# Streaming encoder step: squares of x summed on TensorE in four groups, roots broadcast without diagonal tiles, first weight block in product order

## The chip, the cores and the metric

The kernel runs on one core of a Trainium2 chip. The metric is the device time of one execution in microseconds (us); smaller is better. TensorE is called PE in the rows, VectorE DVE, ScalarE ACT, GpSimd POOL, and SP is the queue from which all of this kernel's transfers are issued. PEld is TensorE's loading of weights, which runs beside its matmuls.

## The reference, cut to what matters

One layer of a hybrid encoder is applied to 512 prompt tokens and 64 sample tokens, all in fp32. The change lies at its very beginning:

```python
mod = jax.nn.silu(c) @ w_ada + b_ada
shift, scale, gate = jnp.split(mod, 3, axis=-1)
h = rmsnorm(x, norm_g) * (1.0 + scale[:, None]) + shift[:, None]
proj = h @ w_in
```

`rmsnorm` divides each token by the root of the mean of its 2048 squares and multiplies by a weight. Attention, a state-space branch, a pooling branch and an output projection follow; the change does not touch them.

## The kernel before, in words

Tokens lie along the free dimension (columns 0 to 511 prompt, 512 to 575 sample: NP = 512, NT = 576), and the 2048 features in 16 blocks of 128 partitions. x arrives transposed, as eight transfers of two blocks each, into four tiles `xc` (line 92).

**The statistics** (lines 349 to 376). The 16 blocks are squared, 15 on ScalarE and the last on VectorE, and VectorE adds them into two tiles `acc`, one for the even and one for the odd blocks. Then ten matmuls (line 373) multiply five stretches of 128 tokens of both `acc` tiles with a column of ones, so that `pss` holds the sum of squares of 128 tokens per column, with the token on the partition. `rms_inv` (line 100) makes the inverse roots `r` of it: one root on ScalarE, the rest small steps on VectorE. Ahead of these matmuls twelve others (`warm`, line 368) multiply a piece of x with the identity; nothing reads their result.

**The broadcast** (lines 387 to 399). A root per partition is needed as a row on every partition. VectorE scales the identity by each column of `r` (tiles `dg`, line 391), five matmuls of ones with `dg` (lines 393 and 395) put the rows into the PSUM tile `rb`, and ScalarE copies them to `rstdx`.

**Modulation** (`ada_mm`, `ada_sel`, `modulate`). For each block b, `ada_mm(b, half)` multiplies SiLU(c) with a half of the block's 1 MB + 1 MB of `w_ada` columns, 16 matmuls in all, into `pa`. `ada_sel(b)` copies `pa` to `S` on ScalarE, transposes it with two matmuls, and reduces it on VectorE to `m4`: shift and scale of prompt and sample. `modulate(b)` forms h from x, `rstdx` and `m4`, splits it into a rounded part `hh` (ScalarE) and a remainder `hl` (VectorE), and keeps the 64 sample columns as `hs`. `split_w(b)` does the same to 768 columns of `w_in`, giving `w1h` and `w1l`.

**The first projection** (`first_tiles`, line 429). For each block, six tiles of output (fA to fD) take three products each, `w1h*hh`, `w1l*hh` and `w1h*hl`, one tile after the other, and four matmuls for the sample tokens go into `fS`. The loop of line 447 interleaves this with the next block: `fS` of block b, `ada_mm(b+1)`, the first tile, `ada_sel(b+1)`, `modulate(b+1)`, the other five tiles. `load_ada` issues the transfers two blocks ahead, in the order of the blocks.

From line 320 to the end of this stage the order on PE, DVE, ACT and SP is the order in which the code is written (`manual_schedule`). What stands in an engine's queue behind a waiting instruction waits too. The rest of the kernel comes out in the same order on every engine with the change and without it.

Of the kernel before, what the change touches and what calls it, by code (L numbers as in the profile page):

```python
# [9 lines left out]
F32 = mybir.dt.float32  # L10
F32R = mybir.dt.float32r
I32 = mybir.dt.int32
AF = mybir.ActivationFunctionType
ALU = mybir.AluOpType
# [3 lines left out]
NP = 512  # L18
NS = 64
NT = NP + NS  # L20
# [17 lines left out]
HELD = 3  # L38
LASTORD = (4, 0, 1, 2, 3)
LASTENG = ("PE", "DVE", "Activation")  # L40
WARM = 12
WLANE = 0
W1POS = 2
SPLIT0 = 1
ORDERED = ("PE", "SP", "DVE", "Activation")
# [3 lines left out]
def kernel(ctx, tc, xp, xs, xT, cT, wada_ss, wada_g, bsh, bsc, bgate, ng, wf1, wrest,  # L49
# [4 lines left out]
    V, A, G, PE, SY = nc.vector, nc.scalar, nc.gpsimd, nc.tensor, nc.sync  # L54
# [3 lines left out]
    wp = ctx.enter_context(tc.tile_pool(name="wp", bufs=3))  # L58
# [4 lines left out]
    def mul(o, a, b):  # L63
        V.tensor_tensor(o, a, b, op=ALU.mult)  # L64

    def add(o, a, b):
        V.tensor_tensor(o, a, b, op=ALU.add)  # L67

    def sub(o, a, b):
        V.tensor_tensor(o, a, b, op=ALU.subtract)  # L70

    def ts(o, a, s1_, s2_, op0, op1):
        V.tensor_scalar(o, a, s1_, s2_, op0=op0, op1=op1)
# [5 lines left out]
    ident = const.tile([128, 128], F32, name="ident")  # L79
# [3 lines left out]
    ones = onesr.bitcast(F32)  # L83
    scT = const.tile([128, KT, 2], F32, name="scT")
# [1 line left out]
    SY.dma_start(cTt, cT)  # L86
    A.activation(scT, cTt, AF.Silu)
    pre = const.tile([128, 1], F32, name="pre")
    A.activation(pre, ones[:, 0:1], AF.Sqrt)
    xc = [ck(f"xc{c}") for c in range(4)]  # L90
    for n in range(8):
        SY.dma_start(xc[n // 2][:, 2 * (n % 2):2 * (n % 2) + 2], xT[n])
# [25 lines left out]
    pp = psctx.enter_context(tc.tile_pool(name="pp", bufs=2, space=PSUM))  # L118
    pm = psctx.enter_context(tc.tile_pool(name="pm", bufs=4, space=PSUM))

    def mtile(name, shape=(128, 512)):
        return pm.tile(list(shape), F32, tag="m", name=name)
# [39 lines left out]
    hh, hl = [], []  # L162
# [161 lines left out]
    def ada_mm(b, half):  # L324
        if half == 0:
            pas[b] = mtile("pa")
        pa = pas[b]
        for k in range(8 * half, 8 * half + 8):
            g = k % 4
            PE.matmul(pa[32 * g:32 * g + 32, 0:256], sc[:, k], adat[b, k // 8][:, k % 8], start=(k < 4),  # L330
                      stop=(k >= KT - 4))

    def ada_sel(b):
        pa = pas.pop(b)
        S = s1.tile([128, 256], F32, tag="S", name="S", bufs=1)
        A.copy(S, pa[:, 0:256])
        for z in range(2):
            PE.transpose(pa[:, 256 + 128 * z:384 + 128 * z], S[:, 128 * z:128 * z + 128], ident)
        m4 = s1.tile([128, 4], F32, tag="m4", name="m4", bufs=4)
        V.tensor_reduce(out=m4.rearrange("p (z t) -> p z t", z=2), op=ALU.add, axis=mybir.AxisListType.X,  # L340
                        in_=pa[:, 256:512].rearrange("p (z g t) -> p z t g", z=2, g=4)[:, :, 0:2])
        V.tensor_scalar(m4[:, 0:2], m4[:, 0:2], prm[:, 0, b:b + 1], None, op0=ALU.add)
        ts(m4[:, 2:4], m4[:, 2:4], prm[:, 1, b:b + 1], prm[:, 2, b:b + 1], ALU.add, ALU.mult)
        m4s[b] = m4
# [1 line left out]
    for b in range(PRE):  # L346
        load_ada(b)

    acc = [wp.tile([128, NT], F32, tag="wh", name="acc") for _ in range(2)]
    for n in range(16):  # L350
        xv = xc[n // 4][:, n % 4]
        if n < 2:
            A.activation(acc[n], xv, AF.Square)
        else:
            sq = wp.tile([128, NT], F32, tag=("wl", "wr")[n % 2], name="sq")
            if n == 15 and 1:
                mul(sq, xv, xv)
            else:
                A.activation(sq, xv, AF.Square)
            if n < 16:  # L360
                add(acc[n % 2], acc[n % 2], sq)
            else:
                acc.append(sq)
    V.tensor_scalar(prm[:, 1], prm[:, 1], 1.0, None, op0=ALU.add)

    warm = pp.tile([128, 2, 512], F32, tag="pj", name="warm")
    for n in range(WARM):
        PE.matmul(warm[:, 0, 0:128], ident, xc[3][:, WLANE, 0:128], start=True, stop=True)
    pss = mtile("pss", (128, 8))
    for t in range(5):  # L370
        t0 = 128 * t if t < 4 else NT - 128
        for n, a in enumerate(acc):
            PE.matmul(pss[:, t:t + 1], a[:, t0:t0 + 128], ones[:, 0:1], start=n == 0, stop=n == len(acc) - 1)
    ada_mm(0, 0)
    ada_mm(0, 1)
    r = rms_inv(s1, pss[:, 0:5], D, None, -0.5 * EPS, [128, 5], "n")
    wsp = {}

# [5 lines left out]
        sub(wl, w, wh.bitcast(F32))  # L384
        wsp[b] = w, wh, wl

    dg = wp.tile([128, 5, 128], F32, tag="wh", name="dg")
    rb = pp.tile([128, 2, 512], F32, tag="pj", name="rb")
    rstdx = s1.tile([128, NT], F32, tag="rstdx", name="rstdx", bufs=1)
    for t in range(5):  # L390
        V.tensor_scalar(dg[:, t], ident, r[:, t:t + 1], None, op0=ALU.mult)
        if t < 4:
            PE.matmul(rb[:, 0, 128 * t:128 * t + 128], ones, dg[:, t], start=True, stop=True)
        else:
            PE.matmul(rb[:, 1, 0:64], ones, dg[:, t, 64:128], start=True, stop=True)
    split_w(0)
    ada_sel(0)
    A.copy(rstdx[:, NP:NT], rb[:, 1, 0:64])
    A.copy(rstdx[:, 0:NP], rb[:, 0])

    fA = pp.tile([128, 2, 512], F32, tag="pj", name="fA")
    fB = pp.tile([128, 2, 512], F32, tag="pj", name="fB")
# [3 lines left out]
    f1p = [fA[:, 0], fA[:, 1], fB[:, 0], fB[:, 1], fC, fD]  # L406
    blk = {}

    def modulate(b):
        m4 = m4s.pop(b)  # L410
        c, i = divmod(b, 4)
        if i == 0:
            hh.append(ck(f"hh{c}", F32R))
            hl.append(ck(f"hl{c}", F32R))
        xv = xc[c][:, i]
        hs = s1.tile([128, 64], F32, tag="hs", name="hs", bufs=3)
        parts = [(0, slice(0, NP)), (1, slice(NP, NT))]
        for t, tk in parts[::-1] if b == 0 else parts:
            stt(xv[:, tk], xv[:, tk], m4[:, 2 + t:3 + t], rstdx[:, tk], ALU.mult, ALU.mult)
            if t:  # L420
                V.tensor_scalar(hs, xv[:, NP:NT], m4[:, 1:2], None, op0=ALU.add)
        for t, tk in parts:
            A.activation(hh[c][:, i, tk], xv[:, tk], AF.Identity, bias=m4[:, t:t + 1])  # L423
        for t, tk in ((0, slice(0, NP)), (1, slice(NP, NT))):
            stt(hl[c][:, i, tk], xv[:, tk], m4[:, t:t + 1], hh[c][:, i, tk].bitcast(F32), ALU.add, ALU.subtract)
        w, wh, wl = wsp.pop(b)
        blk[b] = w, wh, wl, hs

    def first_tiles(b, fs):
        w, wh, wl, hs = blk[b]  # L430
        c, i = divmod(b, 4)
        f0, l0 = b == 0, b == KT - 1
        for f in fs:
            if f < 6:
                wsl = slice(128 * f, 128 * f + 128)
                PE.matmul(f1p[f], wh[:, wsl], hh[c][:, i, 0:NP], start=f0, stop=False)
                PE.matmul(f1p[f], wl[:, wsl], hh[c][:, i, 0:NP], start=False, stop=False)
                PE.matmul(f1p[f], wh[:, wsl], hl[c][:, i, 0:NP], start=False, stop=l0)
            else:

                for g in range(4):
                    PE.matmul(fS[32 * g:32 * g + 32], hs[:, 32 * (g // 2):32 * (g // 2) + 32],
                              w[:, 384 * (g % 2):384 * (g % 2) + 384], start=f0, stop=l0, skip_group_check=True)

    modulate(0)
    dg_ = disc()
    for b in range(KT):
        if b + PRE < KT:
            load_ada(b + PRE)
        if b + 1 < KT:  # L450
            split_w(b + 1)
        if b == KT - 2:
            for n in range(3):
                w_load()
        first_tiles(b, F1CUT[0])
        if b + 1 < KT:
            ada_mm(b + 1, 0)
            ada_mm(b + 1, 1)
        first_tiles(b, F1CUT[1])
        if b + 1 < KT:  # L460
            ada_sel(b + 1)
            modulate(b + 1)
        if b == KT - 2:
            for n in range(1):
                w_split()
        first_tiles(b, F1CUT[2])
        if b == 0:
            ssm_load()
        for _ in range(DISCN if b >= 2 else 0):
            next(dg_, None)  # L470
    for n in range(0):
# [8 lines left out]
    for f in range(6):  # L480
        PE.matmul(fT[:, 64 * f:64 * f + 64], SS[:, 128 * (f % 3):128 * (f % 3) + 128], i2[:, f // 3], start=True,
                  stop=True)
# [512 lines left out]
    for f in range(4):  # L995
        wh, wl = w_next(4)
# [19 lines left out]
        else:  # L1016
            sq = s5.tile([128, NT], F32, tag="tB", name="sq2")
# [42 lines left out]
    for t in range(5):  # L1060
        n = 128 if t < 4 else 64
# [139 lines left out]
    ws = [w_next(2) for _ in range(HELD)]  # L1201
# [3 lines left out]
    with tc.manual_schedule(engines={getattr(mybir.EngineType, e) for e in LASTENG}):  # L1205
        r = {}
# [155 lines left out]
```

## Time and profile before

| what | value |
|---|---|
| median of 3 runs | 1035.28 us (1035.24 to 1037.51) |
| the profiled execution, its own time | 1035.37 us |
| its span in the profile | 1033.1 us |
| TensorE busy | 97% of the span |
| VectorE busy | 69% |
| ScalarE busy | 45% |
| DMA busy, first tenth of the span | over 90% |

The span runs from the first to the last instruction; the execution's own time is 2.3 us longer, which lies outside it. Times in rows count from the start of the span. A row of the timeline has the start, the time that it covers, engine, line, operation, output and inputs, shapes, the number of instructions merged into it (xN), and in brackets how long its engine had been idle before and what released it. An fp32 matmul is recorded as two instructions. In a table by stretches, PEclk is the clock that TensorE was granted, as a share of 2.4 GHz.

### The profile page before, as it was taken

Reading aid. Unit: us, or ns where it says so; the run is one execution under the profiler, and the core shown is the slowest. Engines: PE = TensorE matmul, PEld = TensorE weight load, DVE = VectorE, ACT = ScalarE, POOL = GpSimd, SP = SyncE. Lnnn points to the kernel's source line nnn. Section 1 sums busy time; section 2 is a strip of 40 time slices with the busy share of each in tenths; the row PEclk is TensorE's granted clock in tenths of the full one; section 3 lists DMA queues with packets and bytes.
Section 4 is the critical chain, followed back from the end, with each engine's and each line's share of the span. In section 5 each row is a group of like instructions: output and inputs, shape, how many; then the busy total and the mean of one; then the engine's idle time right before and its main releaser. Section 6 shows DMA issues by size and latency. Waiting matters only on the chain. (4 is left out here: it accounts for less than half of the span.)

```text
span 1033.1 us, 17910 instructions
## 1 busy us (share of the span) xinstructions
PE 1003.0 (97%) x7048; PEld 905.1 (88%) x7048; DVE 710.7 (69%) x1678; ACT 460.3 (45%) x913; POOL 4.2 (0%) x36
## 2 busy tenths in 40 slices
PE   4999999999999999999999999999999999999996
PEld 3666689999999999999989999999999888888885
DVE  5677785745555564644599798886354679988776
ACT  5332365635454544543744454557452514232325
POOL 0000000000000000000000000000000000000000
PEclk9999999999999999999999999999999999999999
DMA  9999552232233333222223222221322585746425
GB/s 366 413 416 369 232 172 86 88 103 87 85 99 94 99 97 95 74 74 75 72 62 91 84 62 86 77 65 51 112 72 87 191 295 195 236 151 197 149 92 194
DMA packets 51571, 148.44 MB, mean 144 GB/s; under 512 B 9312, under 2 KB 18528, under 8 KB 46816
## 3 DMA queue, kind: packets, MB, share of 16 engines
q1 hardware_dynamic: 51488, 147.31, 42.5%
q8 instruction: 55, 0.90, 0.3%
q14 instruction: 28, 0.23, 0.1%
HBM read 137.75 MB, written 9.53 MB: 143 GB/s over the span
## 5 line engine op out<-in xcount | busy, mean ns | idle before, releaser
L500 PE MATMUL pj<-hh,wh 128*128 128x288 f32 x1344 | 299.0, 304 | 0.0
L500 PE MATMUL pj<-hh,wl 128*128 128x288 f32 x1344 | 287.8, 296 | 0.0
L500 PE MATMUL pj<-hl,wh 128*128 128x288 f32 x1344 | 287.4, 295 | 0.0
L500 PEld LDWEIGHTS pj<-hh,wh 128*128 128x128 f32 x1344 | 214.5, 189 | 4.9 <-issue 0.8
L500 PEld LDWEIGHTS pj<-hh,wl 128*128 128x128 f32 x1344 | 216.0, 188 | 0.1
L500 PEld LDWEIGHTS pj<-hl,wh 128*128 128x128 f32 x1344 | 215.6, 188 | 0.1
L146 ACT CAST wh<-w 128x1024 fp32r<-128x1024 f32 x120 | 125.8, 1049 | 198.0 <-PE po L1122 89.4
L70 DVE TENSOR_TENSOR wl<-w,wh 128x1024 fp32r<-128x1024 f32 x120 | 146.7, 1223 | 93.9 <-ACT wh L146 92.9
L1119 PE MATMUL po<-wl,yh 128*128 128x512 f32 (+1 forms) x256 | 99.1, 387 | 0.0
L1120 PE MATMUL po<-wh,yl 128*128 128x512 f32 (+1 forms) x256 | 99.0, 387 | 0.0
L1118 PE MATMUL po<-wh,yh 128*128 128x512 f32 (+1 forms) x256 | 98.7, 387 | 0.0
L76 DVE SCALAR_TENSOR_TENSOR acc<-ada,scT,acc 128x512 f32<-128x512 f32 x120 | 82.9, 744 | 0.5
L621 ACT ACTIVATE P<-P,s 128x128 f32<-128x128 f32 (+4 forms) x80 | 43.3, 541 | 77.2 <-DVE s L620 76.9
L618 DVE CUSTOM_DVE_ANT_0 P<-sps,Tb 128x128 f32<-128x128 f32 (+4 forms) x80 | 36.6, 458 | 36.5 <-PE sps L614 22.4
L1119 PEld LDWEIGHTS po<-wl,yh 128*128 128x128 f32 x256 | 48.1, 188 | 9.9
L1118 PEld LDWEIGHTS po<-wh,yh 128*128 128x128 f32 x256 | 48.1, 188 | 9.9
L1120 PEld LDWEIGHTS po<-wh,yl 128*128 128x128 f32 x256 | 48.1, 188 | 9.8
L622 DVE RECIPROCAL s<-s 128x1 f32<-128x1 f32 (+1 forms) x80 | 12.8, 161 | 43.1 <-ACT P L621 42.4
L623 DVE TENSOR_SCALAR P<-P,s 128x128 f32<-128x128 f32 (+4 forms) x80 | 29.5, 370 | 2.3
L423 ACT ACTIVATE hh<-xc,m 128x512 fp32r<-128x512 f32 (+1 forms) x32 | 15.4, 529 | 34.4 <-DVE xc L76 34.4
L67 DVE TENSOR_TENSOR ssqa<-ssqa,sq 128x576 f32<-128x576 f32 x7 | 5.3, 757 | 35.7 <-ACT sq L666 35.7
L70 DVE TENSOR_TENSOR K<-kv,K 64x704 fp32r<-64x704 f32 x32 | 28.3, 883 | 0.6
(338 smaller groups left out, 1423.6 us busy)
## 6 DMA issues: line engine op xcount, KB each, us to landing
w<-in_wrest_dram SPq DMA_DIRECT2D x84, 512.0 KB, 3.7
ada<-in_wada_ss_dram SPq DMA_DIRECT2D x22, 1024.0 KB, 8.6
w<-in_wout_dram SPq DMA_DIRECT2D x32, 512.0 KB, 3.7
ada<-in_wada_g_dram SPq DMA_DIRECT2D x32, 512.0 KB, 4.3
adac<-in_wada_ss_dram SPq DMA_DIRECT2D x10, 1024.0 KB, 13.8
w<-in_wf_dram SPq DMA_DIRECT2D x16, 384.0 KB, 11.0
xc<-in_xT_dram SPq DMA_DIRECT2D x8, 576.0 KB, 7.3
Tb<-in_ext_dram SPq DMA_DIRECT2D x8, 512.0 KB, 3.6
```

What stands on the lines that cost most here:

```text
L70: V.tensor_tensor(o, a, b, op=ALU.subtract)
L76: V.scalar_tensor_tensor(o, in0=a, scalar=s, in1=b, op0=op0, op1=op1)
L146: A.copy(wh, t)
L423: A.activation(hh[c][:, i, tk], xv[:, tk], AF.Identity, bias=m4[:, t:t + 1])
L500: PE.matmul(ps[:, ch, 0:HC], ws[:, k % 8], hs[c][:, i, HC * ch:HC * ch + HC], start=(k == 0 and first), stop=(k == KT - 1 and last))
L618: V.tensor_tensor_reduce(out=p[0:n, 0:nk], in0=ps[0:n], in1=Tb[0:n, h, ::-1][:, b0:b0 + nk], scale=1.0, scalar=-3.0e38, op0=ALU.add, op1=A ...
L621: A.activation(p[0:n, 0:nk], p[0:n, 0:nk], AF.Exp, bias=s4[0:n, 1:2], accum_out=s4[0:n, 2:3])
L622: V.reciprocal(s4[0:n, 3:4], s4[0:n, 2:3])
L623: V.tensor_scalar(p[0:n, 0:nk], p[0:n, 0:nk], s4[0:n, 3:4], None, op0=ALU.mult)
L1118: PE.matmul(po[t], yh[c][:, ci, s_], wh[:, i], start=f0, stop=False)
L1119: PE.matmul(po[t], yh[c][:, ci, s_], wl[:, i], start=False, stop=False)
L1120: PE.matmul(po[t], yl[c][:, ci, s_], wh[:, i], start=False, stop=l0)
```

## The change

- `acc` is made four times, once for each `xc` tile: the first block of a group is squared into it, the three others are added. After each group five matmuls add its sums into `pss`, which stays open over the four groups.
- The twelve `warm` matmuls of 128 columns go. In their place stand seven of 512 columns that multiply the identity with ones (`FILL`, `WARM`): five ahead of the first group's matmuls, one ahead of the second's, one ahead of the third's.
- The early root that brings in ScalarE's table (`pre`) reads `scT` in place of `ones`.
- `dg` goes. The matmuls to `rb` take a column of `r`, repeated 128 times, as weights and the identity as the moving side.
- The second half of block 0's `ada_mm` moves behind these matmuls. VectorE multiplies block 0 of x by `rb` straight from PSUM; ScalarE's copies to `rstdx` follow, then `ada_sel(0)`, then `split_w(0)`.
- Block 0 has its own `modulate`, in which ScalarE applies scale and shift in one step from the product, and its own `first_block`: all six `w1h*hh`, then `fS` and `ada_mm(1)`, then all six `w1l*hh`, then `ada_sel(1)` and `modulate(1)`, then all six `w1h*hl`.

```diff
-WARM = 12
-WLANE = 0
+FILL = 4
+WARM = (5, 1, 1, 0)
...
-    A.activation(pre, ones[:, 0:1], AF.Sqrt)
+    A.activation(pre, scT[:, 0, 0:1], AF.Sqrt, scale=0.0)
...
-    acc = [wp.tile([128, NT], F32, tag="wh", name="acc") for _ in range(2)]
-    for n in range(16):
...
+    pss = mtile("pss", (128, 8))
+    warm = pp.tile([128, 2, 512], F32, tag="pj", name="warm")
+    for n in range(0, 16, 4):
+
+        for w in range(WARM[n // 4]):
+            PE.matmul(warm[:, 0, 0:128 * FILL], ident, ones.unsqueeze(1).to_broadcast([128, FILL, 128]), start=True,
+                      stop=True)
+        acc = wp.tile([128, NT], F32, tag="wh", name="acc")
+        for m in range(n, n + 4):
+            xv = xc[m // 4][:, m % 4]
+            if m == n:
+                A.activation(acc, xv, AF.Square)
+                continue
+            sq = wp.tile([128, NT], F32, tag=("wl", "wr")[m % 2], name="sq")
+            if m == 15:
+                mul(sq, xv, xv)
+            else:
+                A.activation(sq, xv, AF.Square)
+            add(acc, acc, sq)
+        for t in range(5):
+            t0 = 128 * t if t < 4 else NT - 128
+            PE.matmul(pss[:, t:t + 1], acc[:, t0:t0 + 128], ones[:, 0:1], start=n + t == 0, stop=n == 12,
+                      skip_group_check=True)
...
     ada_mm(0, 0)
-    ada_mm(0, 1)
     r = rms_inv(s1, pss[:, 0:5], D, None, -0.5 * EPS, [128, 5], "n")
...
-        V.tensor_scalar(dg[:, t], ident, r[:, t:t + 1], None, op0=ALU.mult)
+        rt = r[:, t:t + 1].to_broadcast([128, 128])
         if t < 4:
-            PE.matmul(rb[:, 0, 128 * t:128 * t + 128], ones, dg[:, t], start=True, stop=True)
+            PE.matmul(rb[:, 0, 128 * t:128 * t + 128], rt, ident, start=True, stop=True)
...
+    ada_mm(0, 1)
+    mul(xc[0][:, 0, 0:NP], xc[0][:, 0, 0:NP], rb[:, 0])
+    mul(xc[0][:, 0, NP:NT], xc[0][:, 0, NP:NT], rb[:, 1, 0:64])
+    A.copy(rstdx[:, 0:NP], rb[:, 0])
+    A.copy(rstdx[:, NP:NT], rb[:, 1, 0:64])
+    ada_sel(0)
     split_w(0)
-    ada_sel(0)
-    A.copy(rstdx[:, NP:NT], rb[:, 1, 0:64])
-    A.copy(rstdx[:, 0:NP], rb[:, 0])
...
+        if b == 0:
+
+            for t, tk in parts:
+                A.activation(hh[c][:, i, tk], xv[:, tk], AF.Identity, scale=m4[:, 2 + t:3 + t], bias=m4[:, t:t + 1])
+            ts(hs, xv[:, NP:NT], m4[:, 3:4], m4[:, 1:2], ALU.mult, ALU.add)
+            ts(xv[:, 0:NP], xv[:, 0:NP], m4[:, 2:3], m4[:, 0:1], ALU.mult, ALU.add)
+            sub(hl[c][:, i, 0:NP], xv[:, 0:NP], hh[c][:, i, 0:NP].bitcast(F32))
+            sub(hl[c][:, i, NP:NT], hs, hh[c][:, i, NP:NT].bitcast(F32))
+            blk[b] = *wsp.pop(b), hs
+            return
...
+    def first_block():
+
+        w, wh, wl, hs = blk[0]
+        for n, (ws, xs_) in enumerate(((wh, hh), (wl, hh), (wh, hl))):
+            for f in range(6):
+                PE.matmul(f1p[f], ws[:, 128 * f:128 * f + 128], xs_[0][:, 0, 0:NP], start=n == 0, stop=False)
+            if n == 0:
+                first_tiles(0, (6,))
+                ada_mm(1, 0)
+                ada_mm(1, 1)
+            if n == 1:
+                ada_sel(1)
+                modulate(1)
```

TensorE's order from the start to the first matmuls of block 0, before (`pss` are the sums of squares, `pa` the modulation, `fS` the sample tokens):

```order
L368 MATMUL warm<-xc_80,ident 128x128 x12
L373 MATMUL pss<-onesr,acc 128x1 x10
L330 MATMUL pa<-ada,sc 32x256 x16
L393 MATMUL rb<-dg,onesr 128x128 x4
L395 MATMUL rb<-dg,onesr 128x64
L338 MATMUL pa<-ident,S 128x128 x2
L442 MATMUL fS<-w_129,hs 32x384 x4
L330 MATMUL pa<-ada,sc 32x256 x16
L436 MATMUL fA<-hh_265,w1h 128x512
```

The same place with the change:

```order
L354 MATMUL warm<-onesr,ident 128x512 x5
L370 MATMUL pss<-onesr,acc 128x1 x5
L354 MATMUL warm<-onesr,ident 128x512
L370 MATMUL pss<-onesr,acc 128x1 x5
L354 MATMUL warm<-onesr,ident 128x512
L370 MATMUL pss<-onesr,acc 128x1 x10
L330 MATMUL pa<-ada,sc 32x256 x8
L391 MATMUL rb<-ident,r 128x128 x4
L393 MATMUL rb<-ident,r 128x64
L330 MATMUL pa<-ada,sc 32x256 x8
L338 MATMUL pa<-ident,S 128x128 x2
L461 MATMUL fA<-hh_264,w1h 128x512 x2
```

The unread matmuls now stand ahead of three of the four groups, half of the modulation behind the broadcast, and block 0 begins with its products in place of `fS`.

The rest of block 0 on TensorE with the change, up to block 1's first rows (the last two; `fS` there reads `hs` of block 1):

```order
L453 MATMUL fS<-w_129,hs 32x384 x4
L330 MATMUL pa<-ada,sc 32x256 x16
L461 MATMUL fA<-hh_264,w1l 128x512 x2
L461 MATMUL fB<-hh_264,w1l 128x512 x2
L461 MATMUL fC<-hh_264,w1l 128x512
L461 MATMUL fD<-hh_264,w1l 128x512
L338 MATMUL pa<-ident,S 128x128 x2
L461 MATMUL fA<-hl_265,w1h 128x512 x2
L461 MATMUL fB<-hl_265,w1h 128x512 x2
L461 MATMUL fC<-hl_265,w1h 128x512
L461 MATMUL fD<-hl_265,w1h 128x512
L453 MATMUL fS<-w_129,hs 32x384 x4
```

Between the transposes of block 1 (L338) and block 1's `fS` six matmuls are left, where before there were fifteen (five tiles with three products each).

ScalarE's order from the root to block 0's `hh`, before:

```order
L106 ACTIVATE s<-v 128x5
L382 CAST w1h<-w_129 128x768
L336 COPY S<-pa 128x256
L398 COPY rstdx<-rb 128x64
L399 COPY rstdx<-rb 128x512
L423 ACTIVATE hh_265<-xc_77,m_254 128x512
```

And with the change:

```order
L106 ACTIVATE s<-v 128x5
L397 COPY rstdx<-rb 128x512
L398 COPY rstdx<-rb 128x64
L336 COPY S<-pa 128x256
L380 CAST w1h<-w_129 128x768
L422 ACTIVATE hh_264<-xc_77,m_251 128x512
```

The copy of `S`, from which the modulation of block 0 is read, now stands behind both copies of the roots, and as built these wait until VectorE has read the same PSUM tile. Two more waits belong to the new code: the fourth group's `acc` takes the buffer of the first, so its first square waits for the first group's `pss` matmuls; and the first unread matmul waits for `ones`, which VectorE writes behind its second addition, as before.

## Rows read from the trace of the kernel before

**Rows 1.** The page: span, and busy time of TensorE.
```profile
span 1033.1 us, 17910 instructions
...
PE 1003.0 (97%) x7048; PEld 905.1 (88%) x7048; DVE 710.7 (69%) x1678; ACT 460.3 (45%) x913; POOL 4.2 (0%) x36
```
**Rows 2.** Busy time by stretch: length, engines, PEclk, DMA share, GB/s.
```profile
18.50:21.30 2.80, 2.54 (x27) 2.44 (x28) 0.69 (x2) 0.00 (x0) 0.00 (x0) 1.00 1.01 413
21.30:24.70 3.40, 3.40 (x34) 1.45 (x33) 2.79 (x11) 0.93 (x2) 0.00 (x0) 0.52 1.02 424
...
34.86:41.92 7.06, 7.06 (x61) 4.67 (x60) 3.80 (x10) 2.74 (x5) 0.00 (x0) 1.00 1.02 419
```
**Rows 3.** Timeline of the front: squares, additions, ones, and the last transfers of x.
```profile
7.11 1.43 DVE L67 TENSOR_TENSOR acc<-acc,sq 128x576 f32<-128x576 f32 x2 [4.15 <-ACT sq L359]
8.46 0.22 DVE L82 TENSOR_SCALAR onesr<-ident 128x128 fp32r<-128x128 f32 x1
8.76 1.28 ACT L89 ACT_TABLE_LOAD   x1
10.16 6.02 ACT L359 ACTIVATE sq<-xc 128x576 f32<-128x576 f32 x10
10.86 6.78 DVE L67 TENSOR_TENSOR acc<-acc,sq 128x576 f32<-128x576 f32 x10 [1.24 <-ACT sq L359]
15.44 0.81 SPq L189 DMA_DIRECT2D ada<-in_wada_ss_dram  x2
18.34 0.76 DVE L67 TENSOR_TENSOR acc<-acc,sq 128x576 f32<-128x576 f32 x1
```
**Rows 4.** The unread matmuls: durations in ns (min/median/max), first and last start.
```profile
L368 PEld LDWEIGHTS warm<-xc,ident x24: 192/333/333, 13.8 to 18.4; 128*128 128x128 f32 x24
```
**Rows 5.** Timeline, TensorE from the sums to block 0.
```profile
19.16 2.17 PE L373 MATMUL pss<-onesr,acc 128*128 128x1 f32 x18 [0.27 <-DVE acc L67]
21.25 3.49 PE L330 MATMUL pa<-ada,sc 128*32 128x256 f32 x32
24.67 1.25 PE L393 MATMUL rb<-dg,onesr 128*128 128x128 f32 x8
27.80 0.85 PE L442 MATMUL fS<-w,hs 128*32 128x384 f32 x8 [1.49 <-DVE hs L421]
28.47 1.91 PE L330 MATMUL pa<-ada,sc 128*32 128x256 f32 x32
34.86 0.85 PE L442 MATMUL fS<-w,hs 128*32 128x384 f32 x8
```
**Rows 6.** Timeline, the steps from sums to modulation, and in block 0 and 1.
```profile
21.36 0.17 DVE L73 TENSOR_SCALAR v<-pss 128x5 f32<-128x5 f32 x1 [2.18 <-PE pss L373]
22.43 0.17 DVE L76 SCALAR_TENSOR_TENSOR r<-s,r 128x5 f32<-128x5 f32 x1
22.63 1.07 DVE L391 TENSOR_SCALAR dg<-ident,r 128x128 f32<-128x128 f32 x5
26.23 0.59 ACT L399 COPY rstdx<-rb 128x512 f32<-128x512 f32 x1
31.12 0.38 PE L338 MATMUL pa<-ident,S 128*128 128x128 f32 x2
31.95 0.28 DVE L73 TENSOR_SCALAR m<-m,prm 128x2 f32<-128x2 f32 x1
33.26 0.25 DVE L421 TENSOR_SCALAR hs<-xc,m 128x64 f32<-128x64 f32 x1
```
**Rows 7.** Groups by form: a product out of PSUM on VectorE, and `hh`.
```profile
L64 DVE TENSOR_TENSOR tm<-po,gt 128x512 f32<-128x512 f32 x16 | 10.6, 688 | 0.4 <-PE po L1120 0.3
L423 ACT ACTIVATE hh<-xc,m 128x512 fp32r<-128x512 f32 x16 | 11.6, 724 | 34.4 <-DVE xc L76 34.4
```
**Rows 8.** Timeline, ScalarE: block 2's weights and `S`.
```profile
34.71 0.83 ACT L382 CAST w1h<-w 128x768 fp32r<-128x768 f32 x1 [0.69 <-DMA w<-in_wf_dram]
37.56 0.37 ACT L336 COPY S<-pa 128x256 f32<-128x256 f32 x1 [2.02 <-PE pa L330]
```

More of the change, by code (lines that the diff above doesn't have):

```diff
@@ L347 @@
         load_ada(b)
-    acc = [wp.tile([128, NT], F32, tag="wh", name="acc") for _ in range(2)]
-    for n in range(16):
[L351 to L356, printed above, removed]
+    pss = mtile("pss", (128, 8))
[12 more added lines that the diff above has]
+            if m == 15:
                 mul(sq, xv, xv)
@@ L359 @@
                 A.activation(sq, xv, AF.Square)
[L360 to L363, printed above, removed]
-    V.tensor_scalar(prm[:, 1], prm[:, 1], 1.0, None, op0=ALU.add)
[L366 to L373, printed above, removed]
+            add(acc, acc, sq)
[3 more added lines that the diff above has]
+                      skip_group_check=True)
+    V.tensor_scalar(prm[:, 1], prm[:, 1], 1.0, None, op0=ALU.add)
     ada_mm(0, 0)
-    ada_mm(0, 1)
     r = rms_inv(s1, pss[:, 0:5], D, None, -0.5 * EPS, [128, 5], "n")
@@ L385, in split_w @@
         wsp[b] = w, wh, wl
-    dg = wp.tile([128, 5, 128], F32, tag="wh", name="dg")
     rb = pp.tile([128, 2, 512], F32, tag="pj", name="rb")
@@ L390 @@
     for t in range(5):
-        V.tensor_scalar(dg[:, t], ident, r[:, t:t + 1], None, op0=ALU.mult)
+        rt = r[:, t:t + 1].to_broadcast([128, 128])
         if t < 4:
-            PE.matmul(rb[:, 0, 128 * t:128 * t + 128], ones, dg[:, t], start=True, stop=True)
+            PE.matmul(rb[:, 0, 128 * t:128 * t + 128], rt, ident, start=True, stop=True)
         else:
-            PE.matmul(rb[:, 1, 0:64], ones, dg[:, t, 64:128], start=True, stop=True)
+            PE.matmul(rb[:, 1, 0:64], rt, ident[:, 64:128], start=True, stop=True)
+    ada_mm(0, 1)
[4 more added lines that the diff above has]
+    ada_sel(0)
     split_w(0)
-    ada_sel(0)
-    A.copy(rstdx[:, NP:NT], rb[:, 1, 0:64])
-    A.copy(rstdx[:, 0:NP], rb[:, 0])
     fA = pp.tile([128, 2, 512], F32, tag="pj", name="fA")
@@ L417, in modulate @@
         parts = [(0, slice(0, NP)), (1, slice(NP, NT))]
-        for t, tk in parts[::-1] if b == 0 else parts:
+        if b == 0:
[7 more added lines that the diff above has]
+            return
+        for t, tk in parts:
             stt(xv[:, tk], xv[:, tk], m4[:, 2 + t:3 + t], rstdx[:, tk], ALU.mult, ALU.mult)
@@ L454 @@
                 w_load()
+        if b == 0:
+            first_block()
+            ssm_load()
+            continue
         first_tiles(b, F1CUT[0])
@@ L466 @@
         first_tiles(b, F1CUT[2])
-        if b == 0:
-            ssm_load()
         for _ in range(DISCN if b >= 2 else 0):
```

## The prediction
> **What bounds the kernel now.** I read the page first: TensorE is busy for 97% of the span [rows 1], so a change at the front counts only by how much earlier or later TensorE's unbroken stream begins. The table by stretches comes next: from 34.86 us, where block 1 begins, a block takes 7.06 us with TensorE busy throughout [rows 2]. Behind that point both programs have one order, so I take as **landmark** the start of block 1's `fS`, 34.86 us [rows 5], and forecast where it goes. The timeline then tells what sets it.
>
> Issues of the queue wait for earlier transfers, eight places back; by the issue at 15.44 us the last piece of x has landed [rows 3]. ScalarE's ten squares end at 16.18, VectorE's ten additions run 0.68 us each and end later, and the last sum is ready at 19.10 [rows 3]. The `pss` matmuls end at 21.33 [rows 5]. In them TensorE is busy but each has one column, and the clock falls to half: 0.52 of 2.4 GHz over 21.30 to 24.70 us, after 1.00 in the stretch before [rows 2]. There block 0's modulation takes 3.49 us; the same 32 rows take 1.91 us at the full clock [rows 5]. The broadcast waits behind it until 24.67, although `dg` was done at 23.70 [rows 5, 6]. The landmark comes 13.53 us after the last `pss`.
>
> **The sums.** Call F the end of the first five unread matmuls and P the end of the last `pss`; P was 21.33.
>
> *When the unread matmuls begin.* `ones` follows VectorE's second addition. In the new order this is block 2's, which could start at 7.11 in the old trace too; 0.68 for it and 0.22 for `ones` [rows 3] give 8.05 us.
>
> *What they cost.* A row of 128 columns took 0.20 us at half clock: 24 starts from 13.8 to 18.4, with weight loads of 333 ns, 192 ns in the last ones [rows 4], so the full clock came after about 4.2 us. (The level is read there from the rows' durations.) A row of 512 columns is four times as long: 0.82 us at half, 0.43 at full; five matmuls are ten rows. With 4.2 us at half (5.1 rows) and 4.9 rows at full, 2.1 us, F is 14.4. All at full it is 12.3, all at half 16.6.
>
> *The wait they bring.* The `pss` rows start 0.112 us apart [rows 5], so a group's ten take 1.1 us, 1.3 to the last result. The fourth group's `acc` waits for the first group's `pss`, until F + 1.3 = 15.7; x would have allowed 13.75. Behind that, squares every 0.6 us and VectorE's two additions, product and addition end 4.2 us later (0.68 a step, 0.76 for the last [rows 3]), and the last five `pss` 1.3 us after that: **P = F + 6.8 = 21.2**. TensorE's own queue is ready sooner (three groups at 1.1 and two unread matmuls at 0.85 reach F + 5.0; the fourth sums come at F + 5.5). So of what the front seemed to offer 0.1 us is left. ScalarE's table load of 1.28 us [rows 3] goes where ScalarE has nothing to do; that and two additions fewer buy time that the wait takes back. If the unread matmuls were no hindrance, P would be set by the last piece of x: 15.44, a square 0.7, two additions and a product, 3.0 together with the last addition, and `pss` 1.3 make 19.75.
>
> *From P to the roots on all partitions.* The small steps from `pss` to `r` took 1.27 us [rows 5, 6]. They now cover the first half of the modulation, 1.0 us at full clock. `dg`, 1.07 us [rows 6], goes; it lay beside TensorE's modulation, so before it cost nothing, and now nothing covers it if it stayed. The ten `rb` rows take some 1.35 us (ten at the `pss` rows' 0.112 and the last's result; 1.41 before, partly at half clock). Weights repeated with step zero have no row; I take the same time, and 0.2 less or more as ends. `rb` is ready at P + 2.67, call it R.
>
> *From R to block 0.* VectorE's two products, 0.69 [rows 7] and 0.28, end at R + 0.95. ScalarE's two copies (0.59 [rows 6] and 0.2) come behind them and `S` behind the copies, at R + 1.65, although the modulation is ready at R + 1.0. No row of before shows both engines reading `rb`; side by side they would put `S` at R + 1.05. I take the waiting, as it is built. The Trainium skill ("PSUM — Partial Sum Buffer", section on bank collisions) says that two engines may not read one bank at the same time and must be kept apart by a semaphore; by it the copies stay behind, otherwise the sum would be 0.6 lower. `S` 0.37 [rows 8], the transposes 0.1 later, and from their start 1.1 us to the modulation [rows 6]: R + 3.25. `hh`, 0.72 [rows 7]: the first product starts at R + 4.05. `split_w(0)` fits in between: its cast on ScalarE ends at R + 2.75, its remainder on VectorE is needed only after `ada_mm(1)`.
>
> *Block 0.* Six products at 0.23, `fS` 0.67, `ada_mm(1)` 1.84, six products: the transposes of block 1 start at R + 9.4. From there `hs` of block 1 takes 2.39 us (31.12 to 33.51 [rows 6]). Before, fifteen matmuls covered this; now six do, 1.4 us, and TensorE stands 0.75 us. `fS` of block 1 starts at R + 11.85.
>
> So the landmark is P + 2.67 + 11.85 = P + 14.5, against P + 13.5 before: the modulation at full clock (1.6 us) and the earlier broadcast are paid out again, since `fS` and `ada_mm(1)`, 2.5 us of work that used to cover `hh` and `hl`, now come after `hh`, and since TensorE stands at the end of the block. 21.2 + 14.5 = 35.7, **0.85 us later**. The extra VectorE work in block 0 lies beside products. The transfers keep their order and are never idle (DMA share 1.01 to 1.02 [rows 2]), so nothing lands earlier or later; the half of `ada` whose buffer is freed later (24.9 against 24.74) is refilled by an issue that waited for a transfer anyway.
>
> The profiled execution took 1035.37 us, 0.09 above the median: 1035.37 + 0.85 = **1036.2 us**. A measurement of this kernel can tell about 0.3%, 3.1 us, from no change.
>
> **Rivals.** *Early full clock.* If TensorE is granted the full clock within 2 us of the first unread matmul, F is about 13.3, P 20.1 and the time 1035.1; the bound by x, P = 19.75, gives 1034.7. For it: the level rose in the old trace under the same kind of work. Against: it took 4.2 us there.
>
> *The clock falls again.* Between the last unread matmul and P there are 2.8 us with only `pss` rows and a wait; after 2.8 us of that the clock fell before [rows 2]. Then `rb` takes 0.9 us more (ten rows at 0.20) and the first half of the modulation sticks out of its cover by 0.5: 1037.6. Against: the new order puts unread matmuls between the groups.
>
> *Stuck at half clock: slower.* If the full clock comes neither with the unread matmuls nor before P, F is 16.6, the three first groups and two unread matmuls take 9.7 us, the last group 2.3, so P is 28.6; with 1.4 for the broadcast the landmark is 44.5 and the time 1045. It decides, against no change, from some 2.3 us beyond my sum: two groups of `pss` (0.9 each more) and half an unread matmul at half clock. The Trainium skill ("TensorE: Matmul & The Clock Gate", section "What's actually happening") says that the throttled state is the default and activity releases it; the rise in [rows 4] and the fall in [rows 2] agree. Against: the same kind of work raised it in [rows 4].
>
> *Faster by over 0.3%.* It has no place: ScalarE casts block 2's weights when they land, 34.71, ahead of `S` of block 2, which stood at 37.56 [rows 8]. So `S` cannot come before 35.54, and the landmark's gain ends at 2.0 us whatever the front does.
>
> **How the numbers follow.** My forecast 0.42; early clock 0.22; the fall 0.25; stuck 0.06; faster beyond the bound 0.03; 0.02 for a lesser loss of the stuck kind, over the bound in half of the cases. The range from 1034.5 to 1038.0 holds the first three with the ends for `rb` and the copies. Faster 0.03, same 0.90, slower 0.07.
>
> **What would show it.** Right: unread matmuls from about 8.05 to 14.4, the fourth `acc` waiting for `pss` to about 15.7, P near 21, `S` behind the copies, the first product some 6.7 us after P, a stand of 0.75 us ahead of block 1's `fS`, and this near 35.7. A wait for weights or modulation transfers in blocks 0 to 2, or `fS` of block 1 more than 2 us earlier, would prove the argument wrong; a changed 7.06 us per block would too.

## The result: slower by 0.57%, and the profile after

| what | before | changed |
|---|---|---|
| median of the runs beside each other | 1036.35 us (1035.24 to 1037.89, 6 runs) | 1042.02 us (1040.87 to 1044.49, 6 runs) |
| the profiled execution, its own time | 1035.37 us | 1040.93 us |
| its span | 1033.1 us | 1038.7 us |

The ratio is 1.0057, 95% interval 1.004 to 1.0073. The forecast was 1036.2 us within 1034.5 to 1038.0: it was wrong, on the slow side.

The engines, from the page of the changed kernel. TensorE is still busy for 97% of the span, as in [rows 1]; the question is again when its unbroken stream starts.

```profile
span 1038.7 us, 17918 instructions
PE 1011.2 (97%) x7058; PEld 907.2 (87%) x7058; DVE 709.2 (68%) x1672; ACT 460.5 (44%) x913; POOL 4.2 (0%) x36
```

The front of the changed kernel in the timeline (start, us covered, engine, line, operation; in brackets the idle time before and what released it); it answers to [rows 5, 6]:

```profile
8.51 6.73 PE L354 MATMUL warm<-onesr,ident 128*128 128x512 f32 x10 [8.51 <-DVE onesr L82]
16.29 0.68 ACT L360 ACTIVATE acc<-xc 128x576 f32<-128x576 f32 x1 [2.48 <-PE pss L370]
20.71 1.28 PE L370 MATMUL pss<-onesr,acc 128*128 128x1 f32 x10 [0.51 <-DVE acc L67]
21.92 1.07 PE L330 MATMUL pa<-ada,sc 128*32 128x256 f32 x16
23.31 2.08 PE L391 MATMUL rb<-ident,r 128*128 128x128 f32 x8 [0.32 <-DVE r L76]
25.18 0.53 PE L393 MATMUL rb<-ident,r 128*128 128x64 f32 x2
25.64 1.50 PE L330 MATMUL pa<-ada,sc 128*32 128x256 f32 x16
26.65 0.58 ACT L397 COPY rstdx<-rb 128x512 f32<-128x512 f32 x1 [4.22 <-DVE xc L64]
27.24 0.39 ACT L336 COPY S<-pa 128x256 f32<-128x256 f32 x1
29.76 1.05 PE L461 MATMUL fA<-hh,w1h 128*128 128x512 f32 x2 [1.64 <-ACT hh L422]
32.45 1.29 PE L453 MATMUL fS<-w,hs 128*32 128x384 f32 x8
36.90 0.38 PE L338 MATMUL pa<-ident,S 128*128 128x128 f32 x2
39.34 0.85 PE L453 MATMUL fS<-w,hs 128*32 128x384 f32 x8 [0.67 <-DVE hs L432]
...
854.22 0.50 PE L1146 MATMUL po<-wl,yh 128*128 128x512 f32 x1 [1.12 <-DVE wl L70]
```

The landmark, block 1's `fS`, starts at 39.34 instead of 34.86: **4.48 us later**, where 0.85 was forecast. Every wait that was forecast is there: the fourth `acc` waits for `pss`, `S` goes behind the copies, TensorE stands 1.64 us ahead of the first product and 0.67 ahead of the landmark. What was not forecast stands in the durations: the `rb` rows take 2.4 us instead of 1.35, and the first products 1.05 us for a pair of rows that takes 0.73 at full clock (below). Stretches of 1 us (PE busy and its instructions, then PEld, DVE, ACT, POOL; then the granted clock, DMA share, GB/s) say why; before, only one such fall stood in the front [rows 2]:

```profile
21.00:22.00 1.00, 1.00 (x13) 0.99 (x17) 0.00 (x0) 0.00 (x0) 0.00 (x0) 1.00 1.01 418
24.00:25.00 1.00, 1.00 (x7) 1.00 (x7) 0.00 (x0) 0.00 (x0) 0.00 (x0) 0.50 1.04 434
28.00:29.00 1.00, 0.12 (x2) 0.00 (x0) 0.74 (x4) 0.46 (x2) 0.00 (x0) 1.00 0.98 410
31.00:32.00 1.00, 1.00 (x4) 0.66 (x2) 1.00 (x3) 0.00 (x0) 0.00 (x0) 0.50 0.90 372
```

The clock falls twice: behind the one-column sums, in `rb`, and again behind the stand ahead of block 0. The remaining 1.1 us of the span (5.6 against 4.5) arises far from the change: TensorE waits 1.12 us for VectorE in the output projection (the last row of the timeline). It waited there 1.17 us in the kernel e3 below too, whose landmark is that of before, and not at all in e2, whose landmark is almost as late as the change's, so the wait doesn't follow from a late landmark; what brings it was not settled.

### The profile page after: what moved, and what is told of

Read it like the earlier page. It is cut to its first block, busy times and chain, and to the rows that moved or that the text cites. A ratio compares the mean times of both kernels' runs of the same rounds, so it can differ in the third digit from the quotient of the medians.

```text
span 1038.7 us, 17918 instructions
## 1 busy us (share of the span) xinstructions
PE 1011.2 (97%) x7058; PEld 907.2 (87%) x7058; DVE 709.2 (68%) x1672; ACT 460.5 (44%) x913; POOL 4.2 (0%) x36
## 6 DMA issues: line engine op xcount, KB each, us to landing
adac<-in_wada_ss_dram SPq DMA_DIRECT2D x10, 1024.0 KB, 11.6
```

## The experiments

Theory A, throughout: the two falls of the clock cost the time; from f1 on also that the one-column matmuls bring the first. The rival B is named in each text: the order of block 0, the new sums, or the waits. P is again the end of the last `pss`, R the end of `rb`. Where no profile is shown, landmark and P are from the same timeline.

**e1: block 0 in the old order.**

```diff
-        if b == 0:
-            first_block()
-            ssm_load()
-            continue
...
+        if b == 0:
+            ssm_load()
```

> The change with block 0 back in the old order: sample tokens and the next block's modulation first, then one tile after the other with three products each; squares, sums and broadcast stay new. Landmark: start of block 1's sample tokens on TensorE, 34.86 us before and 39.34 us with the change. Theory A (the clock: of the 4.5 us that the landmark lost, some 3 are two stretches of 3.3 and 3.4 us at half clock, the rest are waits): TensorE still idles ahead of block 0, the clock still falls once there, only the stand of 0.7 us before block 1 goes: landmark 38.5 to 39.0, time 0.5 us under the change. Rival B (the product order itself costs: work that used to cover hh and hl now comes behind them): landmark about 37.0, time 2 to 2.5 us under the change.

Ratio 1.0046 (1.0029 to 1.0063). Landmark 40.33, later than in the change, not earlier: neither guess held. Its P was 23.45, and the clock was low over 21.0 to 27.8 and again over 31.2 to 34.7. A landmark alone mixes P, clock and order; from here on I count from P and look at the clock of each stretch. Two falls remain without the product order, so the order does not bring them.

**e2 and e3: the change cut in two.** e2 has the old squares, sums and twelve unread matmuls with all the rest new; e3 is the kernel before with only the new squares, sums and unread matmuls (the first half of the diff ahead).

> The change with the squares, the sums and the twelve narrow unread matmuls of before; broadcast and block 0 stay new. Theory A (clock): the last sums end at 21.3 instead of 22.0, the clock falls near there as it did before, and again in the idle stretch ahead of block 0: landmark 38.5, time 0.7 us under the change. Rival B (the new sums are what costs, by their waits and by what they do to the clock): landmark at 36 or below, time 3 us or more under the change.

> The kernel before with the new squares, sums and wide unread matmuls alone; broadcast over diagonal tiles and block 0 as before. Both theories have the last sums at 22.0 (21.3 before). Theory A: all of the modulation stands behind the sums, dense enough to bring the clock back before block 0, so the landmark is some 0.7 us later than before, 35.6, and the time 1036 to 1037.5 beside 1036.3 before. Rival B (the new sums cost by themselves): landmark 37 or later, time 2 us or more above before.

e2: ratio 1.0033 (1.002 to 1.0046), landmark 38.76, low clock over 22.3 to 25.7 and 29.1 to 32.5, as theory A had it. e3: 1.0007 (0.9991 to 1.0023), landmark 34.82 against 34.86, one fall. (It was expected at 35.6, because P was put at 22.0 and came at 21.32.) So the new front by itself changes nothing that counts, and the loss lies in what follows P. The profile of e3 is still 2.8 us longer than that of before: 1.4 arise about the wait in the output projection, and 1.4 about a fall of the clock near 698 us:

```profile
699.00:700.00 1.00, 1.00 (x6) 1.00 (x5) 1.00 (x2) 0.09 (x1) 0.00 (x0) 0.50 0.00 0
```

This is a part of the program that no kernel here alters. The profile of before does not fall there, though TensorE stands 2.00 us just ahead in it as well:

```profile
697.52 1.21 PE L735 MATMUL bps<-ssqp,onesr 128*128 128x288 f32 x4 [2.00 <-DVE ssqp L67]
```

**e4: the gaps filled,** the one-column sums kept: unread matmuls ahead of the last sums, behind each half of the modulation, and three of 256 columns ahead of block 0 (`fill(n, c)` writes n of them, 128 times c columns wide).

```diff
-WARM = (5, 1, 1, 0)
+WARM = (5, 1, 1, 1)
...
     ada_mm(0, 0)
+    fill(1, 2)
...
     ada_mm(0, 1)
+    fill(1, 2)
...
     ada_sel(0)
+    fill(3, 2)
```

> The change with more unread matmuls, where TensorE waits: one of 512 columns ahead of the fourth group's sums, one of 256 columns behind each half of block 0's modulation, three of 256 columns behind its transposes. Theory A (clock): full clock from the sums to block 1; broadcast 1.0 us and block 0 some 1.8 us shorter, 0.4 us lost to the new matmuls: landmark 36.5 to 37.0, time 2.3 to 2.8 us under the change. Rival B (waits and order, not the clock): landmark 39.3 to 39.8, time the same as the change or up to 0.5 us more.

Ratio 1.0048 (1.0032 to 1.0064), landmark 40.89: later than either theory had it. The first fall came earlier and lasted over 21.0 to 27.9, and in it the two matmuls added ahead of `rb` themselves ran at half clock; the second was gone. In e1, which adds none, the first fall was as long (21.0 to 27.8), so it is not shown that the added matmuls made it longer; they did not prevent it either. The next runs change the sums instead.

**f1 and f2: the sums 96 columns wide.** The same sums, in 96 equal columns of which one is read; f2 also has the three unread matmuls ahead of block 0.

```diff
-    pss = mtile("pss", (128, 8))
+    pss = mtile("pss", (128, 5, 96))
...
-            PE.matmul(pss[:, t:t + 1], acc[:, t0:t0 + 128], ones[:, 0:1], start=n + t == 0, stop=n == 12,
+            PE.matmul(pss[:, t], acc[:, t0:t0 + 128], ones[:, 0:96], start=n + t == 0, stop=n == 12,
...
-    r = rms_inv(s1, pss[:, 0:5], D, None, -0.5 * EPS, [128, 5], "n")
+    r = rms_inv(s1, pss[:, :, 0], D, None, -0.5 * EPS, [128, 5], "n")
```

> The change with the matmuls of the sums 96 columns wide in place of one (96 equal columns, the first is read), so that TensorE multiplies in them instead of only loading weights; the rows stay bound by the weight load, 0.11 us apart. Theory A (the clock falls because of the narrow rows and the idle time near them): the clock no longer falls at the sums, the broadcast takes 1.35 us in place of 2.4, the fall in the idle stretch ahead of block 0 may stay: landmark (start of block 1's sample tokens, 39.34 with the change) 37.0 to 38.3, time 1 to 2.3 us under the change. Rival B (waits and order, whatever the clock): landmark as with the change, 39.3.

> The same, with three more unread matmuls of 256 columns between block 0's transposes and its first products, where TensorE idles 1.6 us. Theory A: full clock from the unread matmuls on to block 1; the last sums at 21.5 to 22, landmark 14.5 us later, the part of waits and order alone: 36.0 to 36.8, time 2.5 to 3.3 us under the change. Rival B: 39.3.

f1: ratio 1.0019 (1.0006 to 1.0032); f2: 1.0011 (0.9997 to 1.0026). The timeline of f1, then its clock in the stretches that fell before:

```profile
21.18 1.35 PE L370 MATMUL pss<-onesr,acc 128*128 128x96 f32 x10 [0.51 <-DVE acc L67]
23.85 1.16 PE L391 MATMUL rb<-ident,r 128*128 128x128 f32 x8 [0.32 <-DVE r L76]
29.23 0.73 PE L461 MATMUL fA<-hh,w1h 128*128 128x512 f32 x2 [1.64 <-ACT hh L422]
37.30 0.85 PE L453 MATMUL fS<-w,hs 128*32 128x384 f32 x8 [0.67 <-DVE hs L432]
```

```profile
23.00:26.00 3.00, 2.68 (x38) 1.66 (x30) 1.47 (x6) 0.00 (x0) 0.00 (x0) 1.00 0.99 411
26.00:29.00 3.00, 0.62 (x6) 0.20 (x2) 1.30 (x5) 2.34 (x5) 0.00 (x0) 1.00 1.04 419
29.00:32.00 3.00, 2.77 (x26) 1.68 (x30) 2.57 (x6) 1.24 (x3) 0.00 (x0) 1.00 0.99 412
```

A wide sum takes hardly longer than a narrow one (1.35 us for ten rows against 1.28), and the clock stays at 2.4 GHz. The landmark comes 2.04 us earlier although P is 0.54 later, with the same stands of 1.64 and 0.67 us. So the stand of 1.64 us does not by itself bring a fall. The ratios of f1 and of the change, 1.0006 to 1.0032 and 1.004 to 1.0073, do not overlap: the wide sums are worth something in the whole time too.

In f2's timeline the landmark is P + 14.78 (P 22.29), where the prediction said P + 14.5. At 37.07 it comes later than the 36.0 to 36.8 expected, and as far behind P as in f1 (14.77): with wide sums the matmuls in the stand gain nothing.

```profile
24.61 0.33 PE L399 MATMUL rb<-ident,r 128*128 128x64 f32 x2
26.92 0.44 PE L338 MATMUL pa<-ident,S 128*128 128x128 f32 x2 [0.97 <-ACT S L336]
29.00 0.73 PE L468 MATMUL fA<-hh,w1h 128*128 128x512 f32 x2 [0.34 <-ACT hh L429]
37.07 0.85 PE L460 MATMUL fS<-w,hs 128*32 128x384 f32 x8 [0.67 <-DVE hs L439]
```

**h1: only the three unread matmuls ahead of block 0,** with the one-column sums of the change.

> The change with its one-column sums as they are, and only the three unread matmuls of 256 columns between the transposes of block 0 and its first products. A (the second half-clock stretch, 30.0 to 33.4 us in the profile of the change, comes from TensorE's standing 1.64 us ahead of block 0, and not from the first stretch): the first stretch stays, some 23 to 26.6, rb takes 2.4 us, the second is gone, and block 1's fS comes 1.5 to 1.8 us earlier than in the change, near 37.7 (P + 15.7); the time is about 1.5 us under the change's. B (the second stretch follows from the first, or from the low share of work in blocks 0's sums before it, and the stand only delays it): the second stretch stays and block 1's fS stays near 39.3 (P + 17.3). C (the clock then stays low from the first stretch on through the fill, as it did with all gaps filled, 21.0 to 27.75): one longer stretch, and fS lies in between, near P + 16.5.

The timeline, then the clock behind the first fall up to the landmark:

```profile
22.72 2.08 PE L397 MATMUL rb<-ident,r 128*128 128x128 f32 x8
27.37 1.46 PE L376 MATMUL warm<-onesr,ident 128*128 128x256 f32 x6
29.17 0.74 PE L468 MATMUL fA<-hh,w1h 128*128 128x512 f32 x2 [0.34 <-ACT hh L429]
37.23 0.85 PE L460 MATMUL fS<-w,hs 128*32 128x384 f32 x8 [0.69 <-DVE hs L439]
```

```profile
26.00:37.20 11.20, 9.41 (x76) 5.82 (x68) 5.63 (x15) 4.42 (x9) 0.00 (x0) 1.00 1.03 410
```

Ratio 1.0044 (1.0028 to 1.006). A held: the first fall stays (`rb` 2.08 for its eight rows), the second is gone (a pair of products 0.74), and the landmark is P + 15.83 (P 21.40), against P + 17.35 in the change. So the second fall costs 1.52 us of the way from P, and the first 1.05 more (15.83 to f2's 14.78). These are differences between single profiles; in the whole time, where the intervals of h1 and of the change overlap, the 1.52 us cannot be seen.

**f3 and f4: the kernel before with one part each.** f3 has the wide sums, f4 the broadcast without `dg`, with the lines that the change has for it.

> The kernel before with the matmuls of the sums 96 columns wide, nothing else. Theory A: the modulation behind the sums runs at full clock, 1.9 us in place of 3.5; the broadcast then waits for the diagonal tiles and starts 2.0 us after the sums in place of 3.3: landmark 33.3 to 33.7 (34.86 before), time 1.2 to 1.5 us under before. Rival B: the broadcast is not what the landmark hangs on; 34.9, no difference.

> The kernel before with the broadcast by repeated weights and no diagonal tiles, nothing else. Both theories: the diagonal tiles lay beside the modulation on TensorE, so landmark and time stay, 34.6 to 34.9. If weights with step zero load slower, the ten rows of the broadcast take more than 1.4 us and the landmark is later by as much: this prices the one operation for which no row stood in the trace of before.

f3: ratio 0.9994 (0.9982 to 1.0006). Its timeline:

```profile
21.72 1.93 PE L330 MATMUL pa<-ada,sc 128*32 128x256 f32 x32
23.58 1.16 PE L393 MATMUL rb<-dg,onesr 128*128 128x128 f32 x8
24.75 0.39 PE L338 MATMUL pa<-ident,S 128*128 128x128 f32 x2
26.62 0.85 PE L442 MATMUL fS<-w,hs 128*32 128x384 f32 x8 [1.49 <-DVE hs L421]
33.67 0.85 PE L442 MATMUL fS<-w,hs 128*32 128x384 f32 x8
```

Without its fall the kernel before takes the modulation in 1.93 us (3.49 in [rows 5]) and reaches the landmark 1.2 us sooner, at P + 11.88 (P 21.79). The eight `rb` rows take 1.16 us, as in f1, whose weights are a repeated column: the repeated weights cost nothing. In f3's whole time the gain of the landmark does not show: its profile falls twice late in the program, which costs 1.0 and 1.5 us there (the last section). f4: 0.9998 (0.9985 to 1.0012), landmark 35.45, later than expected because P is (21.97); its `rb` fell into the half clock and took 2.08. From P the landmark is 13.48 us away, against 13.53 before: `dg` gone is worth nothing there.

**g1, g2, g4: the order, priced without falls.** g4 is f2 with block 0 in the old order. g2 is f2 with the fourth sums in a buffer of their own and `S` ahead of the copies:

```diff
-        acc = wp.tile([128, NT], F32, tag="wh", name="acc")
+        acc = wp.tile([128, NT], F32, tag="wh", name="acc") if n < 12 else rstdx
...
+    ada_sel(0)
     A.copy(rstdx[:, 0:NP], rb[:, 0])
     A.copy(rstdx[:, NP:NT], rb[:, 1, 0:64])
-    ada_sel(0)
```

g1 is meant to be the best of both: the kernel before with the grouped squares, wide sums, that buffer, three unread matmuls ahead of the first sums in place of five, the first half of block 0's modulation ahead of the last sums, and no `dg`.

> The change with wide sums and a filled gap (landmark 37.07), and block 0 in the old order. At full clock the prediction's price of the product order is a stand of 0.7 us before block 1, less 0.25 us by which the sample tokens wait for hs: landmark 36.3 to 36.7. If the product order costs more than that by itself, 35.5 or below; if nothing, 37.1.

> The change with wide sums and a filled gap (landmark 37.07), and in addition the fourth group's sums in a buffer of their own and the copy S ahead of the two copies of the roots: the two waits of my prediction, priced there at about 0.7 us each. If they cost what the prediction says, the last sums come 0.6 to 0.8 us earlier and S 0.6 us earlier after the broadcast: landmark 35.6 to 36.0, time 1.2 us less than that kernel. If the waits are hidden by something else (TensorE's queue, the modulation), the landmark stays at 36.5 to 37.1.

> The kernel before with those parts that cost nothing or gained: squares and sums in four groups (the fourth in a buffer of its own, so that it waits for no sums), sums 96 columns wide, three unread matmuls of 512 columns at the start and one ahead of the second and of the third group, the first half of block 0's modulation ahead of the last sums, broadcast by repeated weights; copies, modulation and block 0 in the order of before. Theory A: full clock throughout, last sums at 20.0 to 20.6, broadcast from 21.9, ten us from there to the landmark: 32.0 to 32.8 (34.86 before, 33.67 with wide sums alone), of which block 2's weights, that land at 34.7 and stand ahead of its modulation on ScalarE, let through at most 2.0 us: time 1.6 to 2.0 us under before. Rival B: landmark and time as with wide sums alone.

g4: ratio 1.0027 (1.0013 to 1.004); landmark 36.69, P 22.69, so P + 14.00 against f2's P + 14.78: the product order costs 0.78 us, about the stand that the prediction put at 0.75. It is made up of 1.02 us more in block 0, the stand among them, less 0.23 us by which block 0 begins earlier.

g2: 1.0009 (0.9994 to 1.0023); P is 20.34, the first product R + 3.57 (R 22.99) against R + 4.06 in f2, the landmark 34.63 or P + 14.29: taking `S` ahead of the copies is worth 0.5 us. The landmark is earlier than the 35.6 to 36.0 expected, by the earlier P. How much of that is the buffer's is not separated, since the unread matmuls came to full speed sooner in that profile.

```profile
24.49 0.44 PE L338 MATMUL pa<-ident,S 128*128 128x128 f32 x2 [0.49 <-ACT S L336]
26.56 0.73 PE L468 MATMUL fA<-hh,w1h 128*128 128x512 f32 x2 [0.34 <-ACT hh L429]
```

g1: 0.9987 (0.9974 to 1.0001), 1035.59 us against 1036.86 beside it. Block 0 begins 2.1 us earlier than before, but of this 0.9 is lost one block on, because the weights of block 1 land late and `S` of block 1 stands behind their cast on ScalarE:

```profile
28.71 0.83 ACT L383 CAST w1h<-w 128x768 fp32r<-128x768 f32 x1 [1.44 <-DMA w<-in_wf_dram]
29.45 0.36 ACT L336 COPY S<-pa 128x256 f32<-128x256 f32 x1
29.86 0.44 PE L338 MATMUL pa<-ident,S 128*128 128x128 f32 x2 [0.72 <-ACT S L336]
33.67 0.85 PE L441 MATMUL fS<-w,hs 128*32 128x384 f32 x8
```

Its landmark is 33.67, that of f3, and not the 32.0 to 32.8 expected. It is the lowest ratio measured here, but the interval reaches 1: no version is shown to beat the kernel before.

All profiles beside each other, by the width of the sums and the order of block 0 (a fall is a stretch in which the granted clock is 0.50):

| kernel | sums | order | P | falls in the front, us | landmark | from P |
|---|---|---|---|---|---|---|
| before | 1 column | old | 21.33 | 21.5 to 24.9 | 34.86 | 13.53 |
| e3 | 1 | old | 21.32 | 22.1 to 25.5 | 34.82 | 13.50 |
| f4 | 1 | old | 21.97 | 23.2 to 26.6 | 35.45 | 13.48 |
| f3 | 96 columns | old | 21.79 | none | 33.67 | 11.88 |
| g1 | 96 | old | 21.30 | none | 33.67 | 12.37 |
| the change | 1 | new | 21.99 | 23.2 to 26.6, 30.0 to 33.4 | 39.34 | 17.35 |
| e2 | 1 | new | 21.55 | 22.3 to 25.7, 29.1 to 32.5 | 38.76 | 17.21 |
| e1 | 1 | block 0 old | 23.45 | 21.0 to 27.8, 31.2 to 34.7 | 40.33 | 16.88 |
| e4 | 1 | new, gaps filled | 24.43 | 21.0 to 27.9 | 40.89 | 16.46 |
| h1 | 1 | new, one gap filled | 21.40 | 22.1 to 25.5 | 37.23 | 15.83 |
| f1 | 96 | new | 22.53 | none | 37.30 | 14.77 |
| f2 | 96 | new, one gap filled | 22.29 | none | 37.07 | 14.78 |
| g2 | 96 | new, one gap filled, `S` early | 20.34 | none | 34.63 | 14.29 |
| g4 | 96 | block 0 old, one gap filled | 22.69 | none | 36.69 | 14.00 |

All eight profiles with one-column sums fall, and none of the six with wide sums. There is one profile of each kernel, and where a fall starts differs between executions of the same instructions (the change, e1 and h1 are alike up to `rb`), so the cost of a single fall is that of one execution.

## Why the prediction was wrong, step by step

| step | forecast | changed kernel |
|---|---|---|
| unread matmuls begin | 8.05 | 8.51 |
| fourth `acc` waits until | 15.7 | 16.29 |
| P | 21.2 | 21.99 |
| `rb` ready, R | P + 2.67 | P + 3.72 |
| first product | R + 4.05 | R + 4.05 |
| transposes of block 1 | R + 9.4 | R + 11.19 |
| stand ahead of block 1 | 0.75 | 0.67 |
| landmark | 35.7 | 39.34 |

**What held.** The path was right: each wait, each releaser and the terms that don't hang on the clock. With the clock undisturbed (f2) the way from P to the landmark is 14.78 us against 14.5. That the first product is R + 4.05 to the hundredth is luck in part: `S` began 0.12 us earlier than forecast (R + 1.53), and the steps behind it took that much longer. The wait of the fourth `acc` came; ScalarE, idle for 4.22 us, began the copies when VectorE's product was done; 7.06 us per block stayed (39.34 to block 2's `fS` at 46.40).

**What failed** is one step: the sum took the full clock from P to the landmark. It priced the ten `rb` rows at "some 1.35 us", and in block 0 a product at 0.23 and `fS` at 0.67. In the changed kernel the `rb` rows took 2.40 us (2.39 to 2.40 in e1, e2 and h1 too, 1.52 in e4, where the fall ended among them), and from the first product to the transposes of block 1 it took 7.14 us where 5.35 was forecast. The miss of the landmark, 3.6 us, is made up of 1.05 (first fall, f2 against h1), 1.52 (second fall, h1 against the change), 0.8 (P) and 0.3 (f2 against the sum). The 0.8 is mostly that execution's: with the same front P came at 21.40 in h1 and at 21.32 in e3. In the changed kernel VectorE reached `ones` at 8.23 in place of 7.79, and the unread matmuls began 0.46 later.

**The rival "the clock falls again"** named the first fall, its place and its price for `rb` (0.9, measured 1.05). Three things were wrong in it. It had a chance of 0.25 although the evidence for it was a row of before, [rows 2], and the evidence against only an intention of the new order. The 0.5 us that it added for the first half of the modulation did not come, for that half still ran at full clock (1.07 us); the second half was slowed, to 1.50 us, and that was hidden, because `S` waits for the copies until 27.24 anyway. And nothing in it said that a second fall may follow: the order moved `fS` and `ada_mm(1)` behind `hh`, and so opened a stand of 1.64 us on TensorE which the sum counted as time alone, not as a risk to the rows behind it.

**Why it is slower and not equal.** Without any fall the new order takes 14.78 us from P (f2) and the old 11.88 (f3), 2.9 more. The two timelines place it: `rb` is ready 0.48 us sooner behind P in f2 (2.65 against 3.13), block 0's first row comes 4.06 us behind R against 1.70, and block 0 takes 8.07 us against 7.05. Nearly all of the middle part lies ahead of block 0's transposes: in the old order they run right behind `rb` (24.75 in f3), since all of the modulation was done by then, and in the new they start 1.98 us behind R (26.92 in f2), after its second half and both copies. Of the whole, 0.78 is the product order (g4) and about 0.5 `S` behind the copies (g2). The kernel before pays 1.65 for its own fall (13.53 against 11.88), the change 1.05 and 1.52. The prediction booked the 1.65 as a gain, and the change did not collect it.

**The size in microseconds.** The change's profiled execution is 4.7 us above the forecast: 3.6 at the landmark and 1.1 from the wait at 854 us. Its median is another 1.1 higher; the median of before, in the runs beside it, is likewise 1.0 above before's profiled execution.

**Two sums of the prediction that don't add up.** P "set by the last piece of x" is given as 19.75, but its terms (15.44, 0.7, 3.0, 1.3) make 20.4, so the lower bound of the first rival, 1034.7, should have been about 0.7 us higher. Ten rows at 0.82 us from 8.05 make F 16.3 at half clock, not 16.6. Neither bears on the miss.

Left open: why a stand of 1.64 us is followed by a fall in the change and not in f1, and 1.48 us ahead of block 0 in e3, where one fall had come before, brings none. The runs show only that work in the stand (h1, e4) or no earlier fall (f1) avoids it.

## What to carry to other kernels

Ask of every stretch of a front not only how long TensorE's rows are but at which clock, and take a fall that a row of the profile shows as the likeliest case for the same instructions in the new order too. A column count of one is no saving where widening the product costs nothing; and work moved out of a wait of TensorE is paid twice, once as time and once as a possible fall behind it. Judge a part of such a change from a point that it moves (P), since the end of the whole carries scatter of the same size.

## What the runs showed of the hardware that was not expected

- **The clock fell behind one-column matmuls though the engine reads busy.** TensorE is busy at 1.00 over 21 to 22 us of the change, and the clock is at 0.50 by 24; with 96 columns in the same ten rows (1.35 against 1.28 us) it stays at 1.00, in six profiles of six against none of eight. The Trainium skill ("TensorE: Matmul & The Clock Gate", section "What's actually happening") has the throttled state as the default that activity lifts. The rows of the change agree: TensorE, idle up to 8.51 us, takes 2.08 us for its first two rows of 512 columns and 1.10 for two such rows at 16.11.
- **At the start the clock column does not show it.** Over 8.6 to 11.6 us of the change the granted clock reads 1.00, while those first rows take about twice as long as the later ones; there the level can only be read from the rows' durations, as the prediction did.
- **The same program falls late in some executions.** Near 526 us the clock fell in 5 of the 14 profiles (e1, f3, f4, g4, h1), near 699 us in 6 (e3, f3, f4, g1, g4, h1), and at neither place in the other seven, before and the change among them. The instructions there are the same in all, behind stands of TensorE of 2.38 and 2.00 us in the profile of before. In e3 one such fall lengthened the program by 1.4 us, in f3 two by 1.0 and 1.5. Such falls may be a part of the scatter of the kernel before, 1034.96 to 1040.32 us in 31 runs; that they are is not shown.
- **A column of weights repeated with step zero loads like any other:** 1.16 us for eight rows in f1 and in f3.
